# Row-wise maximum of absolute values over 8192 x 8192: groups of 48 and 16 rows per partition instead of 46 and 18, and the second group's results in one store

## The chip, the cores and the metric

The kernel runs on one core of a Trainium2 chip. The metric is the device time of one execution in microseconds (us), of which the median of several executions is taken. A profiled execution has a time of its own, and inside it a span from the first to the last instruction.

## The reference

```
x = randn(8192, 8192), float32
out = np.linalg.norm(x, ord=np.inf, axis=1)      # 8192 float32
```

For two-dimensional input with an axis given this is, for each row, the largest absolute value in the row: `out[i] = max over j of |x[i, j]|`. The input has 268.44 MB, the output 32 KiB. There is one comparison per element read, so the input passes through the core once and nothing is used twice.

## The kernel before

**Layout.** The 8192 rows are spread over 128 partitions, 64 rows to a partition. They are not spread in one piece: `GROUPS = [46, 18]` (L18) makes two groups. The first 46 x 128 rows of x belong to group one, where partition p holds the 46 neighbouring rows 46p to 46p+45; the last 18 x 128 rows belong to group two, with 18 neighbouring rows to a partition. The views are made at L47 to L50: `x_of` is a [128, k x 8192] view of x and `out_of` a [128, k] view of the output. A row has 8192 x 4 bytes = 32 KiB, so from one partition to the next a load moves on in memory by 46 x 32 KiB = 1472 KiB in group one and by 18 x 32 KiB = 576 KiB in group two. This distance is called the pitch below.

**Loads.** The 64 rows of a partition are taken in order, in the pieces that WHOLE (L21) and LAST (L24) list: two loads of one row (8192 elements for each partition), 29 of two rows (16384 elements, 64 KiB for each partition, 8 MiB in all), one of two rows and one of one row whose work is shared among engines, and then the last row in six pieces from 3920 down to 352 elements. All 39 loads are issued by SP at L108, in this order, into a ring of three 64 KiB places (RING, L27), the last piece into a tile of its own (`last`). A load waits until VectorE has finished with the place of the ring that it overwrites.

**Work.** VectorE (DVE) reduces each buffer with one `tensor_reduce` with absolute value and maximum (L68), which writes one or two columns of `res`, a [128, 64] tile with one column for each row of a partition. Towards the end (L133 to L136 and L146 to L150) a part of each buffer goes another way: ScalarE (ACT) replaces it by its absolute value in place (L90), and GpSimd (POOL) takes its maximum as integers (L75). The partial results are then joined, on POOL for rows 61 and 62 (L136), and on DVE for the last row (L153), which reads the last 352 elements and the nine partial results together.

**Stores.** After the last reduce three stores are issued. SP stores the last column alone, 4 bytes for each partition (L154, `final`). ACT stores columns 0 to 45 (184 bytes for each partition) and columns 46 to 62 (68 bytes for each partition) at L159; these two stand behind ACT's own absolute values in its queue. The dependency at L160 orders only the schedule, so that the early stores take the later semaphores; it adds no wait.

**Order.** `keep` holds each engine's instructions in program order. SP's queue has only the loads and then the final store.

Of the kernel before, what the change touches and what calls it, by code (L numbers as in the profile page):

```python
# [1 line left out]

# [4 lines left out]

P = 128
FP32 = mybir.dt.float32
INT32 = mybir.dt.int32  # L10
MAX = mybir.AluOpType.max
X = mybir.AxisListType.X
ABS = mybir.ActivationFunctionType.Abs

GROUPS = [46, 18]  # L18


WHOLE = (  # L21
    [(8192, ())] * 2 + [(16384, ())] * 29 + [(16384, (3712, 3680)), (8192, (2016, 1984))]
)
LAST = [  # L24
    (3920, (1680,)), (1984, (848,)), (1040, (432,)), (576, (240,)), (320, ()), (352, ())
]
RING = 3 * 16384  # L27


@with_exitstack  # L30
def kernel(
    ctx: ExitStack,
    tc: tile.TileContext,
    x: bass.AP,
    out: bass.AP,
):
    nc = tc.nc
    n_rows, n_cols = x.shape
    R = n_rows // P
    assert R == sum(GROUPS) and n_cols == 8192  # L40
    keep = tc.keep_in_program_order


    first = []
    x_of, out_of = {}, {}
    for k in GROUPS:
        f = len(first)  # L47
        x_of[f] = x[f * P : (f + k) * P].rearrange("(p r) m -> p (r m)", r=k)
        out_of[f] = out[f * P : (f + k) * P].rearrange("(p r) -> p r", r=k)
        first += [f] * k  # L50

    single = ctx.enter_context(tc.tile_pool(name="single", bufs=1))

    ring = single.tile([P, RING], FP32)
    res = single.tile([P, R], FP32)

    n_parts = sum(1 + len(g) for w, g in LAST[:-1])
    last = single.tile([P, LAST[-1][0] + n_parts], FP32)

    def not_before(inst, other, why):  # L60
        tc.add_manual_dep(
            inst.ins, other.ins.name,
            mybir.DependencyInfo(mybir.DependencyClass.Sync, mybir.DependencyReason.DATA),
            reason=why,
        )

    def absmax(dst, src):
        return keep(nc.vector.tensor_reduce(  # L68
            out=dst, in_=src, axis=X, op=MAX, apply_absolute_value=True,
        ))  # L70

    def max_pool(dst, src):

        pool = nc.gpsimd
        keep(pool.add_instruction(  # L75
            mybir.InstTensorReduce(
                name=nc.get_next_instruction_name(),
                ins=[pool.lower_ap(src.bitcast(INT32))],
                outs=[pool.lower_ap(dst.bitcast(INT32))],
                op=MAX,  # L80
                axis=X,
            )
        ))

    def shared(part, buf, g):

        a = buf.shape[1] - sum(g)
        red = absmax(part[:, :1], buf[:, :a])
        for i, c in enumerate(g):
            keep(nc.scalar.activation(buf[:, a : a + c], buf[:, a : a + c], ABS))  # L90
            max_pool(part[:, 1 + i : 2 + i], buf[:, a : a + c])
            a += c
        return red

    loads = []

    def load(pos, w):

        row = pos // n_cols
        a = pos - first[row] * n_cols  # L100
        if pos + w == R * n_cols:
            buf = last[:, :w]
        else:
            at = loads[-1][0] + loads[-1][1] if loads else 0
            if at + w > RING:
                at = 0
            buf = ring[:, at : at + w]
        inst = nc.sync.dma_start(out=buf, in_=x_of[first[row]][:, a : a + w]).ins  # L108
        if pos + w < R * n_cols:
            if (len(loads) + 4) % 10 < 5:  # L110


                for b, v, earlier in loads:
                    if b < at + w and at < b + v:
                        tc.declare_no_dep(
                            inst, earlier, reason="ordered by the reduces in between",
                        )
            loads.append((at, w, inst))
        return buf


    pos = 0
    for u, (w, g) in enumerate(WHOLE):
        buf = load(pos, w)
        row, k = pos // n_cols, w // n_cols
        pos += w
        whole = k - 1 if g else k
        if whole:
            red = absmax(
                res[:, row : row + whole],  # L130
                buf[:, : whole * n_cols].rearrange("p (c m) -> p c m", m=n_cols),
            )
        if g:  # L133
            part = single.tile([P, 1 + len(g)], FP32, name=f"part{u}")
            shared(part, buf[:, whole * n_cols :], g)
            max_pool(res[:, row + whole : row + k], part)  # L136
        if u == 1:

            not_before(
                keep(nc.scalar.activation(res[:, :1], res[:, :1], ABS)),  # L140
                red, "not before the second row is in",
            )


    n = LAST[-1][0]
    for h, (w, g) in enumerate(LAST[:-1]):  # L146
        buf = load(pos, w)
        pos += w
        shared(last[:, n : n + 1 + len(g)], buf, g)
        n += 1 + len(g)  # L150

    load(pos, LAST[-1][0])
    absmax(res[:, R - 1 :], last)  # L153
    final = nc.sync.dma_start(out=out_of[first[-1]][:, GROUPS[-1] - 1 :], in_=res[:, R - 1 :])  # L154


    for f, o in out_of.items():
        k = min(o.shape[1], R - 1 - f)
        early = keep(nc.scalar.dma_start(out=o[:, :k], in_=res[:, f : f + k]))  # L159
        tc.add_manual_dep(  # L160
            early.ins, final.ins.name,
            mybir.DependencyInfo(
                mybir.DependencyClass.NoSync, mybir.DependencyReason.SCHED_ONLY
            ),
            reason="takes the later semaphore",
        )


# [1 line left out]
_INS = ['x']  # L170
_OUTS = [((8192,), 'float32')]


# [23 lines left out]
```

## Time and profile before

| | us |
|---|---|
| median of 4 runs (627.40 to 627.47) | 627.42 |
| the profiled execution, its own time | 627.38 |
| its span, first to last instruction | 625.6 |
| outside its span | 1.78 |
| DVE busy | 536.7 |
| ACT busy | 15.1 |
| POOL busy | 14.1 |

The page gives each engine's busy time and its share of the span, the DMA queues with the bytes that they moved, a chain of waits followed back from the last instruction, groups of instructions with the mean time of one and the idle time before them, and for DMA issues the time from issue to landing. Queue q1 is SP's, q10 is ACT's. The landing time of a load holds the time that it stood behind earlier loads. A table by stretches of time gives busy time, DMA share and GB/s for each stretch; a DMA share of 1.00 says that all 16 DMA engines were busy throughout.

### The profile page before, as it was taken

Reading aid. Unit: us, or ns where it says so; the run is one execution under the profiler, and the core shown is the slowest. Engines: PE = TensorE matmul, PEld = TensorE weight load, DVE = VectorE, ACT = ScalarE, POOL = GpSimd, SP = SyncE. Lnnn points to the kernel's source line nnn. Section 1 sums busy time; section 2 is a strip of 40 time slices with the busy share of each in tenths; the row PEclk is TensorE's granted clock in tenths of the full one; section 3 lists DMA queues with packets and bytes.
Section 4 is the critical chain, followed back from the end, with each engine's and each line's share of the span. In section 5 each row is a group of like instructions: output and inputs, shape, how many; then the busy total and the mean of one; then the engine's idle time right before and its main releaser. Section 6 shows DMA issues by size and latency. Waiting matters only on the chain.

```text
span 625.6 us, 175 instructions
## 1 busy us (share of the span) xinstructions
DVE 536.7 (86%) x40; ACT 15.1 (2%) x10; POOL 14.1 (2%) x14
## 2 busy tenths in 40 slices
DVE  1938988889888899888898888988889888899888
ACT  0000000000000000000000000000000000000044
POOL 0000000000000000000000000000000000000026
DMA  8999999999999999999999999999999999999997
GB/s 369 436 469 402 469 402 469 402 469 402 469 402 448 423 406 465 402 469 402 469 402 469 402 469 402 469 402 440 432 402 469 402 469 402 469 402 469 402 436 304
DMA packets 6048, 268.47 MB, mean 429 GB/s; under 512 B 1056, under 2 KB 1312, under 8 KB 1696
## 3 DMA queue, kind: packets, MB, share of 16 engines
q1 hardware_dynamic: 5760, 268.44, 99.3%
q10 hardware_dynamic: 288, 0.03, 0.0%
HBM read 268.44 MB, written 0.03 MB: 429 GB/s over the span
## 4 chain that ended last, share of the span: by engine, by line
DMA 71%; DVE 28%; SPq 0%; issue 0%; DVEq 0%
DMA ring<-in_x_dram 71%; DVE res L68 28%; DVE last L68 1%; SPq L108 0%; DVEq L68 0%
## 5 line engine op out<-in xcount | busy, mean ns | idle before, releaser
L68 DVE TENSOR_REDUCE res<-ring 128x2 f32<-128x16384 f32 (+1 forms) x32 | 525.4, 16420 | 86.3 <-DMA ring<-in_x_dram 86.3
L90 ACT ACTIVATE ring<-ring 128x3712 f32<-128x3712 f32 (+7 forms) x8 | 13.6, 1719 | 577.2 <-DMA ring<-in_x_dram 573.9
L75 POOL TENSOR_REDUCE part<-ring 128x1 int32<-128x3712 int32 (+3 forms) x4 | 10.1, 2561 | 607.6 <-ACT ring L90 607.6
L68 DVE TENSOR_REDUCE part<-ring 128x1 f32<-128x800 f32 (+1 forms) x2 | 5.5, 2748 | 0.1
L68 DVE TENSOR_REDUCE last<-ring 128x1 f32<-128x2240 f32 (+4 forms) x5 | 5.3, 1115 | 0.1
L75 POOL TENSOR_REDUCE last<-ring 128x1 int32<-128x1680 int32 (+3 forms) x4 | 3.4, 854 | 0.6 <-ACT ring L90 0.4
L140 ACT ACT_TABLE_LOAD x1 | 1.3, 1283 | 0.7 <-PEq L181 0.7
L140 ACT ACTIVATE res<-res 128x1 f32<-128x1 f32 x1 | 0.2, 203 | 29.2 <-DVE res L68 29.2
L68 DVE TENSOR_REDUCE res<-last 128x1 f32<-128x361 f32 x1 | 0.5, 529 | 0.1
L75 POOL TENSOR_REDUCE res<-part 128x1 int32<-128x3 int32 x2 | 0.4, 197 | 0.1
L181 POOL MEMSET const-float32-0.0<- 128x1 f32 x1 | 0.1, 98 | 0.2 <-issue 0.2
L181 POOL MEMSET const-bfloat16-1.0<- 128x1 bf16 x1 | 0.1, 101 | 0.0
L181 POOL MEMSET const-uint8-127<- 128x1 uint8 x1 | 0.1, 101 | 0.0
L181 POOL MEMSET const-float32-1.0<- 128x1 f32 x1 | 0.1, 98 | 0.0
## 6 DMA issues: line engine op xcount, KB each, us to landing
ring<-in_x_dram SPq DMA_DIRECT2D x3, 4096.0 KB, 21.3
ring<-in_x_dram SPq DMA_DIRECT2D x1, 1960.0 KB, 35.4
ring<-in_x_dram SPq DMA_DIRECT2D x1, 992.0 KB, 37.4
ring<-in_x_dram SPq DMA_DIRECT2D x1, 520.0 KB, 38.2
ring<-in_x_dram SPq DMA_DIRECT2D x30, 40.8
ring<-in_x_dram SPq DMA_DIRECT2D x1, 288.0 KB, 38.4
last<-in_x_dram SPq DMA_DIRECT2D x1, 176.0 KB, 38.3
ring<-in_x_dram SPq DMA_DIRECT2D x1, 160.0 KB, 38.3
```

The source lines that it names most:

```text
L68: return keep(nc.vector.tensor_reduce(out=dst, in_=src, axis=X, op=MAX, apply_absolute_value=True,))
L75: keep(pool.add_instruction(mybir.InstTensorReduce(name=nc.get_next_instruction_name(), ins=[pool.lower_ap(src.bitcast(INT32))], outs=[poo ...
L90: keep(nc.scalar.activation(buf[:, a : a + c], buf[:, a : a + c], ABS))
L140: keep(nc.scalar.activation(res[:, :1], res[:, :1], ABS)),
L181: nc = _bacc.Bacc("TRN2", target_bir_lowering=False, num_devices=1)
```

## The change

The groups become 48 and 16 rows for each partition. The pitch of a load becomes 48 x 32 KiB = 1536 KiB in group one and 16 x 32 KiB = 512 KiB in group two. The list of loads, the ring and all reduces keep their sizes; only which rows of x a partition holds, and so the addresses in memory, are others. The border between the groups lies behind row 47 of a partition instead of behind row 45.

The three stores become two. SP stores all 16 columns of the second group after the last reduce, 64 bytes for each partition, which lie one after another in the output without a gap (8 KiB). ACT stores the 48 columns of the first group, 192 bytes for each partition. The store of columns 46 to 62 is gone.

```diff
-GROUPS = [46, 18]
+GROUPS = [48, 16]
...
     load(pos, LAST[-1][0])
     absmax(res[:, R - 1 :], last)
-    final = nc.sync.dma_start(out=out_of[first[-1]][:, GROUPS[-1] - 1 :], in_=res[:, R - 1 :])
 
 
-    for f, o in out_of.items():
-        k = min(o.shape[1], R - 1 - f)
-        early = keep(nc.scalar.dma_start(out=o[:, :k], in_=res[:, f : f + k]))
-        tc.add_manual_dep(
-            early.ins, final.ins.name,
-            mybir.DependencyInfo(
-                mybir.DependencyClass.NoSync, mybir.DependencyReason.SCHED_ONLY
-            ),
-            reason="takes the later semaphore",
-        )
+
+    f, g = first[0], first[-1]
+    final = nc.sync.dma_start(out=out_of[g], in_=res[:, g:])
+    early = keep(nc.scalar.dma_start(out=out_of[f], in_=res[:, f:g]))
+    tc.add_manual_dep(
+        early.ins, final.ins.name,
+        mybir.DependencyInfo(mybir.DependencyClass.NoSync, mybir.DependencyReason.SCHED_ONLY),
+        reason="takes the later semaphore",
+    )
```

## The prediction

> **What bounds the kernel now.** I read the page from the top first: busy times, the DMA queues, the chain of waits.
>
> ```profile
> span 625.6 us, 175 instructions
> DVE 536.7 (86%) x40; ACT 15.1 (2%) x10; POOL 14.1 (2%) x14
> ...
> q1 hardware_dynamic: 5760, 268.44, 99.3%
> q10 hardware_dynamic: 288, 0.03, 0.0%
> ...
> DMA ring<-in_x_dram 71%; DVE res L68 28%; DVE last L68 1%; SPq L108 0%; DVEq L68 0%
> ```
>
> VectorE is busy for 86% of the span, but the packets of SP's queue fill 99.3% of the time of 16 DMA engines. The chain changes between a load and a reduce because a load needs a free place in the ring; which of the two is the bound is seen in the groups of instructions, kept apart by shape:
>
> ```profile
> L68 DVE TENSOR_REDUCE res<-ring 128x2 f32<-128x16384 f32 x29 | 499.4, 17220 | 70.3 <-DMA ring<-in_x_dram 70.3
> ```
>
> A two-row reduce takes 17.22 us, and each waits some 2.1 us for its load. Reduces follow one another every 19.35 us, at the loads' pace. The table by stretches, three reduces to a stretch, gives that pace in three stretches of group one (46 rows) and then in the stretch that holds the first loads of group two (18 rows):
>
> ```profile
> 117.17:175.22 58.05, 51.66 (x3) 0.00 (x0) 0.00 (x0) 1.00 1.00 434
> 175.22:233.27 58.05, 51.66 (x3) 0.00 (x0) 0.00 (x0) 1.00 1.00 434
> 233.27:291.32 58.05, 51.66 (x3) 0.00 (x0) 0.00 (x0) 1.00 1.00 434
> ...
> 466.10:524.15 58.05, 51.66 (x3) 0.00 (x0) 0.00 (x0) 1.00 1.00 434
> ```
>
> Three loads are 3 x 8.389 MB = 25.17 MB in 58.05 us, 433.5 GB/s, with a DMA share of 1.00. The two-row reduces start at 41.87 us with row 2 and go on by 19.35 us a pair, so that rows 46 and 47, group two's first, are reduced from 41.87 + 22 x 19.35 = 467.6 us. The rate is the same on both sides. So the kernel is a stream at one rate from start to end, and then a tail, which the timeline shows:
>
> ```profile
> 621.11 1.10 ACT L90 ACTIVATE ring<-ring 128x432 f32<-128x432 f32 x2 [0.37 <-DMA ring<-in_x_dram]
> 621.81 0.86 ACTq L159 DMA_DIRECT2D out_dram<-res  x2
> 622.80 0.53 DVE L68 TENSOR_REDUCE res<-last 128x1 f32<-128x361 f32 x1
> 623.35 0.35 SPq L154 DMA_DIRECT2D out_dram<-res  x1
> ```
>
> The last reduce ends at 623.33, SP issues the last store at 623.35, and the span ends at 625.6. The list of DMA issues gives the three stores' times to landing:
>
> ```profile
> out_dram<-res ACTq DMA_DIRECT2D x1, 23.0 KB, 1.6
> out_dram<-res ACTq DMA_DIRECT2D x1, 8.5 KB, 1.6
> out_dram<-res SPq DMA_DIRECT2D x1, 0.5 KB, 1.4
> ```
>
> The last one lands at 623.35 + 1.4 = 624.75; the remaining 0.85 us is the program's closing.
>
> **What the Trainium skill says.** Four places bear on this, all in "DMA: Bandwidth & Descriptors".
> - "Where 436 GB/s comes from" puts the ceiling of the 16 ports at 435.2 GB/s. The trace agrees: 433.5, and a DMA share of 1.00.
> - "Latency and other measured facts" has a row on the row pitch at large powers of two. Copies from memory to memory of [128 x 16 KiB] tiles ran at 214 GB/s in each direction when the pitch was padded by 4 KiB, at 207 with a pitch of 512 KiB, at 164 with 2 MiB and 103 with 4 MiB. It calls the cause (streams in lock step meeting in the same channels) an inference. The trace of before can neither confirm nor deny it: its pitches are 1472 KiB = 23 x 64 KiB and 576 KiB = 9 x 64 KiB, neither a large power of two, and both run at 434.
> - "The descriptor swizzle" gives each engine blocks of four neighbouring partitions, so that neighbouring engines read four pitches apart. No view here shows it.
> - "Specifications" has transfers below 512 B done by reading and rewriting. All stores here, before and after, are below that (4, 68 and 184 bytes; then 64 and 192), so the page offers no gain to the 64 bytes.
>
> **The change, part by part.**
>
> *Loads with another pitch.* The 39 loads, their bytes, their order and SP's waits stay as they are; no instruction is added or moved here. What may change is the rate. The pitch becomes 1536 KiB = 3 x 512 KiB for 48 of the 64 rows and 512 KiB for 16, so all the traffic now has 512 KiB as the power of two in its pitch, where before it had 64 KiB. Nothing covers a loss: DVE already waits 2.1 us for each load, so a load that takes longer lengthens the run by the whole difference. The stream is 268.44 MB / 433.5 GB/s = 619.2 us, so one per cent of rate is 6.2 us. The upper end comes from the skill's row: 214/207 = 1.034, that is 0.034 x 619.2 = +20.9 us. The lower end: the rate may rise at most from 433.5 to the stated 435.2, 0.4%, -2.4 us. I take 0. The reason is that the row's loss is for copies, in which the same engines read and write memory at the same pitch; at 2 MiB they still moved 164 + 164 = 328 GB/s in both directions together and at 512 KiB 414, with both sides aliased. A load has only its reading side in memory, half as many streams, and at 512 KiB the row's loss has almost faded. Against this: 414 is less than the 434 that the load needs, so the row doesn't exclude a loss, and I give that nearly the same chance.
>
> *The border behind row 47.* One load of rows 46 and 47 comes from group one instead of two. No load crosses a border. 0.
>
> *Reduces.* Same shapes, same number, other rows: 0. DVE's 17.22 us against 19.35 us covers 2.13 us anyway.
>
> *ACT's stores, two to one.* The two issues take 0.86 us of ACT's queue from 621.81; one remains, so ACT is done some 0.43 us earlier (622.24). Nothing stands behind it. The stores landed by 622.24 + 1.6 = 623.8 at the latest, before SP's at 624.75. Off the path: 0. One store fewer must be waited for at the close; the closing semaphore steps on SP take 17 to 28 ns each, so at most -0.03 us.
>
> *SP's store, 4 to 64 bytes for each partition.* It waits for the same last reduce; it now waits also for POOL's results for rows 61 and 62, the later of which is in at 618.47 + 0.20 = 618.67, 4.7 us before. Nothing stands behind it on SP. As before it has 128 pieces, so the issue of 0.35 us stays. Its time to landing is bounded by the rows that surround it: 1.4 us at 4 bytes and 1.6 at 68 and 184, so 0 to +0.2. A gain below zero would need 64 bytes to land sooner than 4; as the landing 1.4 is mostly fixed, I let it go to -0.1. I take +0.1.
>
> *Sum.* On the profiled execution's own time: 627.38 (span 625.6 and 1.78 outside) + 0 + 0.1 = 627.48, rounded to 627.5. The profiled execution lies 0.04 below the median of 627.42, which is less than the rounding.
>
> **Rivals.**
>
> *Part of the pitch's loss shows (slower).* Place: every load. If a copy's 3.4% is the sum of what its two aliased sides lose, a load loses 1.7%: 0.017 x 619.2 = 10.5 us, 637.9 us. For it: the DMA engines have no slack (share 1.00), and all 39 loads have the pitch. Against: the two directions of a copy may disturb one another, which a load doesn't know. It decides as soon as memory gives the 16 engines less than 433.5 GB/s together; above that it is worth nothing.
>
> *The whole of it or more (slower).* If memory gives only what the copies had in both directions together at 512 KiB, 414 GB/s or a little more, the loss is 3.4 to 4.7%. With the row's ratio: 627.4 + 20.9 = 648.3 us. For it: 64 KiB are read in one piece from each partition, so streams remain in step for long. Against: as above.
>
> *Faster stream.* The new addresses let the rate reach 435.2: 627.4 - 2.4 = 625.0 us. Against: nothing in the trace shows a rate that depends on the pitch, and 0.4% is all there is.
>
> *The tail turns out otherwise.* The 64-byte store could land 0.2 later or 0.1 sooner: 627.3 to 627.6. This stays within the forecast.
>
> **How the numbers follow.** A difference of 0.2% (1.25 us) is about what a measurement of this kernel can tell from no change. Only the tail moves: 0.48, 627.5 us. Part of the loss: 0.26, around 637.9, from 629 to 643. The whole or more: 0.23, around 648.3 and beyond. Faster stream: 0.03. So faster 0.03, same 0.48, slower 0.26 + 0.23 = 0.49. The likeliest case has the range 626.9 to 628.4 of its own: from -0.1 in the landing and a rate better by 0.07%, to +0.2 and a rate worse by 0.1%. The range for 8 in 10 begins at 626.9, which leaves out the faster stream, and must reach into the third case: up to 648.3 it leaves out half of that, 0.115, so 0.145 in all. The slower cases together hold as much as the likeliest; they are spread over 20 us, which it is not.
>
> **What would show it.** The stretches of three reduces: 58.05 us and 434 GB/s if the pitch costs nothing; 59.0 and 426 in the second case; 60.0 and 419 in the third. DVE's wait before a two-row reduce: 2.13 us, against 2.46 and 2.79. If the two pitches differ, the stretch length jumps at row 48, 41.87 + 23 x 19.35 = 486.9 us. In the tail, the distance from the end of the last reduce to the end of the span: 2.27 us now, 2.2 to 2.5 expected; SP's store 1.4 to 1.6 to landing, and one ACT store. The prediction is wrong if the stretches are longer than 58.2 us with a DMA share of 1.00, or if a wait of SP on something other than the reduces appears between loads.

## The result and the profile after

The changed kernel takes 628.15 us (median of 34 runs, 627.93 to 628.49) against 627.44 us for the kernel before (52 runs, 627.34 to 627.73). The ratio is 1.0011, with a 95% interval of 1.0006 to 1.0016: slower by 0.7 us. This is clear of the noise, though it is less than the 0.2% that the prediction took for about the least that can be told from no change. The profiled execution took 628.23 us with a span of 626.5 us; before it was 627.38 and 625.6. So there are 0.9 us of span to be found.

The page after, its head and the queues:

```profile
span 626.5 us, 174 instructions
DVE 536.7 (86%) x40; ACT 15.0 (2%) x10; POOL 14.1 (2%) x14
...
q1 hardware_dynamic: 5760, 268.45, 99.3%
q10 hardware_dynamic: 144, 0.02, 0.0%
```

The work is the same; q10, ACT's queue, has half the packets because one of its two stores is gone. The first place to look is the rate. These are the same stretches of time as in the prediction (length, then busy time and count of DVE, ACT and POOL, clock, DMA share, GB/s):

```profile
117.17:175.22 58.05, 51.66 (x4) 0.00 (x0) 0.00 (x0) 1.00 1.00 434
175.22:233.27 58.05, 51.66 (x4) 0.00 (x0) 0.00 (x0) 1.00 1.00 434
233.27:291.32 58.05, 51.65 (x4) 0.00 (x0) 0.00 (x0) 1.00 1.00 434
466.10:524.15 58.05, 51.66 (x4) 0.00 (x0) 0.00 (x0) 1.00 1.00 434
```

434 GB/s in both groups, as before. (A count of x4 only says that a stretch cuts reduces at both ends.) The end of the run is as long as before: from the end of the last reduce, 624.18, to the end of the span there are 2.3 us, before 2.27.

```profile
623.65 0.53 DVE L68 TENSOR_REDUCE res<-last 128x1 f32<-128x361 f32 x1
624.20 0.35 SPq L158 DMA_DIRECT2D out_dram<-res  x1
```

The list of DMA issues shows the two stores, KB and us to landing:

```profile
out_dram<-res ACTq DMA_DIRECT2D x1, 24.0 KB, 1.5
out_dram<-res SPq DMA_DIRECT2D x1, 8.0 KB, 1.4
```

Sixteen times as many bytes land in the same 1.4 us. What is left is the start. The timeline of VectorE, before (start, duration, instruction, idle time ahead of it and what ended it):

```profile
12.83 8.69 DVE L68 TENSOR_REDUCE res<-ring 128x1 f32<-128x8192 f32 x1 [12.83 <-DMA ring<-in_x_dram]
22.51 8.69 DVE L68 TENSOR_REDUCE res<-ring 128x1 f32<-128x8192 f32 x1 [1.00 <-DMA ring<-in_x_dram]
41.87 17.22 DVE L68 TENSOR_REDUCE res<-ring 128x2 f32<-128x16384 f32 x1 [10.67 <-DMA ring<-in_x_dram]
```

and after:

```profile
13.58 8.69 DVE L68 TENSOR_REDUCE res<-ring 128x1 f32<-128x8192 f32 x1 [13.58 <-DMA ring<-in_x_dram]
23.26 8.69 DVE L68 TENSOR_REDUCE res<-ring 128x1 f32<-128x8192 f32 x1 [1.00 <-DMA ring<-in_x_dram]
42.62 17.22 DVE L68 TENSOR_REDUCE res<-ring 128x2 f32<-128x16384 f32 x1 [10.68 <-DMA ring<-in_x_dram]
62.09 17.22 DVE L68 TENSOR_REDUCE res<-ring 128x2 f32<-128x16384 f32 x1 [2.25 <-DMA ring<-in_x_dram]
```

The first load lands 13.58 - 12.83 = 0.75 us later, and the second and third are late by the same 0.75. The fourth adds 2.25 - 2.13 = 0.12. The last reduce starts at 623.65 instead of 622.80, 0.85 later: nothing further is lost in 560 us. The whole difference is made by the first four loads, nearly all of it by the very first, and it is never won back, because the stream behind it has no slack.

The packet records of the two traces, which hold start, duration and size of each piece that a DMA engine moved, narrow this down. A packet of the first load carries the 32 KiB of one partition, and the first sixteen packets all begin before any of them has ended. The last of these sixteen ends at 3.97 us before and at 4.73 after. That is 0.76 us later, so the whole delay of the first load is already there at the end of its first packets.

**Theory:** the new pitch costs a fixed amount while the stream starts and nothing once it runs. A possible reason is that the 16 DMA engines begin in step, meet in memory at such a pitch, and drift apart. **Rivals:** the stores cost it; or the pitch costs whenever the engines come to it; or it costs a little all the time.

### The profile page after: what moved, and what is told of

Its sections match the earlier page's. It is cut to its first block, busy times and chain, and to the rows that moved or that the text cites. A ratio compares the mean times of both kernels' runs of the same rounds, so it can differ in the third digit from the quotient of the medians.

```text
span 626.5 us, 174 instructions
## 1 busy us (share of the span) xinstructions
DVE 536.7 (86%) x40; ACT 15.0 (2%) x10; POOL 14.1 (2%) x14
## 4 chain that ended last, share of the span: by engine, by line
DMA 71%; DVE 28%; SPq 0%; issue 0%; DVEq 0%
DMA ring<-in_x_dram 71%; DVE res L68 28%; DVE last L68 1%; SPq L108 0%; DVEq L68 0%
## 5 line engine op out<-in xcount | busy, mean ns | idle before, releaser
L90 ACT ACTIVATE ring<-ring 128x3712 f32<-128x3712 f32 (+7 forms) x8 | 13.6, 1719 | 577.3 <-DMA ring<-in_x_dram 574.0
```

## The experiments

Each cut shows what a kernel has in place of the changed kernel's lines, except in the second experiment, which starts from the kernel before. In kernels with other groups SP stores the last group at the end and ACT each other group with a store of its own; the lines for this are left out of the cuts.

**The stores alone.** The groups stay 46 and 18; the stores are those of the change.

```diff
-GROUPS = [48, 16]
+GROUPS = [46, 18]
```

> Groups of 46 and 18 as before, stores as after (one store of the second group at the end, 72 bytes per partition here). Theory: the 0.7 us are lost in the first loads, through the pitch; so this is as before, 627.4 (within 0.1), and the third load's reduce starts at 41.9. Rival: the later or bigger last store costs it; then 628.1.

627.46 us against 627.40 for before on the same chip, ratio 1.0001 (0.9993 to 1.0009). The first reduce starts as early as in the kernel before, and the last store lands in 1.4 us:

```profile
12.73 8.69 DVE L68 TENSOR_REDUCE res<-ring 128x1 f32<-128x8192 f32 x1 [12.73 <-DMA ring<-in_x_dram]
```

```profile
out_dram<-res SPq DMA_DIRECT2D x1, 9.0 KB, 1.4
```

The stores are not the cause.

**The groups alone.** Before's three stores, with the new groups.

```diff
-GROUPS = [46, 18]
+GROUPS = [48, 16]
```

> Groups of 48 and 16, three stores as before (last column alone). Theory (pitch, in the first loads): as after, 628.1, the third load's reduce starts at 42.5 or later, stretches of three reduces stay 58.05. Rival (stores): 627.4.

628.08 us, ratio 1.0011 (1.0004 to 1.0017): all of the change's cost. The first reduce is late by 0.57, the fifth waits 2.31 instead of 2.13:

```profile
13.40 8.69 DVE L68 TENSOR_REDUCE res<-ring 128x1 f32<-128x8192 f32 x1 [13.40 <-DMA ring<-in_x_dram]
...
81.33 17.22 DVE L68 TENSOR_REDUCE res<-ring 128x2 f32<-128x16384 f32 x1 [2.31 <-DMA ring<-in_x_dram]
```

The third load's reduce starts at 42.45, a little before the 42.5 that was expected.

**512 KiB in the first 16 rows alone.**

```diff
-GROUPS = [48, 16]
+GROUPS = [16, 30, 18]
```

> Groups of 16, 30 and 18 rows: pitch 512 KiB for the first 16 rows alone, then 960 KiB = 15 x 64 KiB and 576 KiB; 18 columns stored at the end. Theory (cold start: only the first loads pay): the first load's reduce starts 0.5 to 0.8 us later than before's 12.83, nothing more is lost later, 628.0 to 628.2. Rival (1536 KiB with its own pattern costs, 512 KiB does not): 627.4.

628.14 us, ratio 1.0011 (1.0005 to 1.0018). The first reduce starts at 13.42, the third load's at 42.47, and every later two-row reduce waits 2.12 to 2.14 us.

```profile
13.42 8.69 DVE L68 TENSOR_REDUCE res<-ring 128x1 f32<-128x8192 f32 x1 [13.42 <-DMA ring<-in_x_dram]
```

So 512 KiB and 3 x 512 KiB cost about the same at the start (0.59 us here, 0.57 and 0.75 above), and a quarter of the rows at that pitch costs as much as all of them.

**1536 KiB from row 14 on.**

```diff
-GROUPS = [48, 16]
+GROUPS = [14, 48, 2]
```

> Groups of 14, 48 and 2 rows: pitch 448 KiB = 7 x 64 KiB for the first 14 rows, 1536 KiB from row 14 on; the last group's two columns are stored at the end. Theory (cold start: the pitch costs only while all engines begin in step): 627.4, third load's reduce at 41.9. Rival (the engines pay once whenever they come to a pitch of a large power of two): the start is as before, some 0.8 us are lost between rows 14 and 20 (120 to 200 us), 628.1. Second rival (steady small loss): stretches over 58.1 from row 14 on, more than 628.1.

628.83 us, ratio 1.0023 (1.0015 to 1.0031), 1.4 more than the theory expected. But the stream did what the theory said. The timeline, first reduce, the first two of rows 14 to 17 and the last one:

```profile
12.81 8.69 DVE L68 TENSOR_REDUCE res<-ring 128x1 f32<-128x8192 f32 x1 [12.81 <-DMA ring<-in_x_dram]
...
157.95 17.22 DVE L68 TENSOR_REDUCE res<-ring 128x2 f32<-128x16384 f32 x1 [2.13 <-DMA ring<-in_x_dram]
177.30 17.22 DVE L68 TENSOR_REDUCE res<-ring 128x2 f32<-128x16384 f32 x1 [2.13 <-DMA ring<-in_x_dram]
...
622.81 0.53 DVE L68 TENSOR_REDUCE res<-last 128x1 f32<-128x361 f32 x1
```

The last reduce starts at 622.81, before's at 622.80. 48 rows at 1536 KiB cost nothing once the stream runs; both rivals on the loads fall. The loss of this kernel is behind the last reduce, in the list of DMA issues:

```profile
out_dram<-res SPq DMA_DIRECT2D x1, 1.0 KB, 2.7
```

A store of 8 bytes for each partition, which lie in the output without gaps, took 2.7 us to landing, where 4 bytes 72 bytes apart had taken 1.4. That was a side effect of the third group, and it needed runs of its own.

**The 8-byte store behind other loads.**

```diff
-GROUPS = [48, 16]
+GROUPS = [46, 16, 2]
```

> Groups of 46, 16 and 2 rows, the last group's two columns stored at the end, 8 bytes per partition without gaps. Theory for the end of the run with groups of 14, 48 and 2 (the store of short neighbouring pieces takes 2.7 us to landing where 4 bytes 72 bytes apart and 64 or 72 bytes without gaps take 1.4): the same 2.7 here, 627.4 + 1.3 = 628.7. Rival (its long landing came from the loads' pitch before it): 1.4 and 627.4. The 512 KiB of rows 46 to 61 cost nothing in either.

628.82 us, ratio 1.0022 (1.0014 to 1.0031), with 2.9 us to landing, so the 1536 KiB ahead of the store was not the cause. In both kernels the last two rows have the pitch 64 KiB, which this pair can't part from the store; a run below does so for 4 bytes.

**32 bytes instead of 8.**

```diff
-GROUPS = [48, 16]
+GROUPS = [46, 10, 8]
```

> Groups of 46, 10 and 8 rows; the last group's eight columns are stored at the end, 32 bytes per partition without gaps. Theory (stores without gaps cost the more, the more partitions fall into one short stretch of memory: 4 bytes 7.5 us, 8 bytes 2.8, 64 bytes 1.4): 1.4 to 2.0 us to landing, 627.4 to 628.0. Rival (anything below 64 bytes without gaps costs over a us): 2.5 us or more, over 628.5.

627.42 us, ratio 1.0000 (0.9991 to 1.0008), 1.4 us to landing. Pieces of 32 bytes side by side are as good as 64 or 72.

**4 bytes side by side, at the end and early.** One group of one row in front.

```diff
-GROUPS = [48, 16]
+GROUPS = [1, 45, 18]
```

> Groups of 1, 45 and 18 rows: the first load has the pitch 32 KiB, without a gap between partitions; then 1440 KiB = 45 x 32 KiB. 18 columns stored at the end. Theory (the cold start is a question of the first load's addresses): if a pitch with a smaller power of two starts better, the first reduce begins before 12.7 and the time is 627.0 to 627.3; if before's start has no loss from the pitch, as before, 627.4. Rival (neighbouring pieces collide more): over 627.6.

633.63 us, ratio 1.0099 (1.0085 to 1.0113): far over the rival's 627.6, and for the most part not in the loads. The start is worse than before's by 0.3 (first reduce at 13.13), and some 6 us are lost in the stores:

```profile
out_dram<-res ACTq DMA_DIRECT2D x1, 22.5 KB, 8.2
out_dram<-res ACTq DMA_DIRECT2D x1, 0.5 KB, 7.6
out_dram<-res SPq DMA_DIRECT2D x1, 9.0 KB, 7.5
```

All three are slow, so the list alone doesn't say which one holds up the others. Moving the 4-byte store ahead does (the cut is against the kernel just shown):

```diff
+            f0 = GROUPS[0]
+            keep(nc.scalar.dma_start(out=out_of[0], in_=res[:, :f0]))
...
-        if f == g:
+        if f in (0, g):
             continue
```

> Groups of 1, 45 and 18 rows again, but the first column's store, 4 bytes per partition without gaps, is issued at some 31 us under the loads and not at the end. Theory (that store's 4-byte neighbours took the 7.5 us at the end of the run, and held up the other two stores): the end is short again, last store 1.4 us to landing, 627.5 to 627.9 (the first reduce at 13.1). Rival (the other stores, 180 and 72 bytes, or the odd pitch are the cause): 7 us or more to landing again, 633.6.

629.66 us, ratio 1.0035 (1.0022 to 1.0048). At the end, the stores land in 1.5 and 1.4 us again, so the 4-byte store was the cause. The expected 627.5 to 627.9 was missed all the same, because under the loads the store is not free. The third and fourth loads' reduces:

```profile
42.91 17.22 DVE L68 TENSOR_REDUCE res<-ring 128x2 f32<-128x16384 f32 x1 [11.35 <-DMA ring<-in_x_dram]
63.87 17.22 DVE L68 TENSOR_REDUCE res<-ring 128x2 f32<-128x16384 f32 x1 [3.73 <-DMA ring<-in_x_dram]
```

They wait 11.35 and 3.73 us, where the kernel with the store at the end had 10.67 and 2.12: 2.3 us of load time lost to a store of 512 bytes. (The profiled execution, 630.05 us, is the slowest of the five.)

**Two rows at 64 KiB in front of 1536 KiB.** The same early store, here with 8 bytes for each partition.

```diff
-GROUPS = [48, 16]
+GROUPS = [2, 48, 14]
```

> Groups of 2, 48 and 14 rows: the first two loads have the pitch 64 KiB, and 1536 KiB begins with the third load. The first group's two columns are stored by ACT at some 31 us, under the loads; 14 columns at the end. Theory (only the first load of all pays for a large power of two): the first reduce starts at 12.7 to 13.2 and nothing is lost at the third load, 627.3 to 627.8. Rival (the engines pay at the first loads of the large pitch, when they still run in step from the start): the third load's reduce starts 0.5 to 0.8 later than the first load's start alone explains, 628.0 to 628.6.

629.13 us, ratio 1.0029 (1.0017 to 1.0040), outside what either theory said. The first reduce starts well, at 12.77; the third load's is late:

```profile
42.96 17.22 DVE L68 TENSOR_REDUCE res<-ring 128x2 f32<-128x16384 f32 x1 [11.79 <-DMA ring<-in_x_dram]
```

It waits 1.12 us longer than before's (10.67). The 8-byte store is issued in the same stretch, at 31.4, and the 4-byte one was just seen to delay the same load. So this run doesn't tell whether the pitch costs something at the third load; it is inconclusive by its own design.

**A larger power of two.** 1024 KiB, then 2048 KiB throughout.

```diff
-GROUPS = [48, 16]
+GROUPS = [32, 32]
```

> Groups of 32 and 32 rows: pitch 1024 KiB throughout, stores as after. Theory: the loss at the start grows with the power of two in the pitch, 1 to 3 us, 628.4 to 630.5, and stretches stay at 58.05 to 58.2. Rival (memory can no longer feed the stream at this pitch): stretches of 59 us and more, 635 to 660.

639.80 us (four runs, 637.98 to 640.38), ratio 1.0192 (1.0178 to 1.0206). This lies in the rival's range, not in the theory's. The stretches are slow first and right at last:

```profile
0.00:46.77 46.77, 17.37 (x2) 1.49 (x2) 0.20 (x4) 1.00 0.99 381
46.77:227.51 180.74, 154.98 (x10) 0.00 (x0) 0.00 (x0) 1.00 1.00 421
227.51:401.66 174.15, 154.97 (x9) 0.00 (x0) 0.00 (x0) 1.00 1.00 432
401.66:575.81 174.15, 154.98 (x9) 0.00 (x0) 0.00 (x0) 1.00 1.00 434
```

The second stretch, 421 GB/s, has a DMA share of 1.00 too: the share says that the engines had packets, not that these moved at full rate. This stretch holds nine reduces, 60.2 us for three, so the rival was right about it. By the last stretch the pitch of 1024 KiB runs at 434, so memory can deliver at it; that the loss fades after the start is nearer to the theory.

```diff
-GROUPS = [48, 16]
+GROUPS = [64]
```

> One group of 64 rows, pitch 2048 KiB throughout; one store of 256 bytes per partition at the end. Theory (the loss grows with the power of two in the pitch: 0.7 us at 512 KiB, 12.4 at 1024): 30 to 150 us over before, 657 to 780, with a loss in every stretch and no longer only at the start. Rival (a load, which has memory on one side only, drifts apart as at 1024 KiB): 640 to 655, the loss in the first third.

639.83 us (four runs, 637.45 to 641.41), ratio 1.0193 (1.0174 to 1.0213). The theory's dose, 657 to 780, is wrong: 2048 KiB costs the same as 1024, at the lower end of the rival's range. But the loss lies elsewhere than in the rival's first third. In the profiled execution, the slowest of the four, the third load's reduce starts 4.7 us later than before's, the last two-row reduce 8.5 later (592.20 against 583.68) and the last reduce of all 13.95 later (636.75 against 622.80). Four stretches up to 569 us have 385, 428, 430 and 431 GB/s, and then the pieces of the last row come late:

```profile
626.52 2.49 DVE L68 TENSOR_REDUCE last<-ring 128x1 f32<-128x2240 f32 x1 [0.53 <-DMA ring<-in_x_dram]
631.12 1.33 DVE L68 TENSOR_REDUCE last<-ring 128x1 f32<-128x1136 f32 x1 [2.11 <-DMA ring<-in_x_dram]
633.58 1.59 DVE L68 TENSOR_REDUCE last<-ring 128x1 f32<-128x608 f32 x3 [1.12 <-DMA ring<-in_x_dram]
636.75 0.53 DVE L68 TENSOR_REDUCE res<-last 128x1 f32<-128x361 f32 x1 [1.58 <-DMA last<-in_x_dram]
```

Before, these reduces followed one another without a wait. The packet records show that the packets themselves are slow here: the 128 packets of the last load, 1408 bytes each, take 0.22 us on average and up to 1.07, against 0.06 in the kernel before and at 1024 KiB. These packets also end far apart, within 7.2 us here against 0.7 before and 1.4 after the change. That alone is not the reason, since at 1024 KiB they end within 7.3 us and the last reduces have no such waits.

**An uneven start at 1024 KiB.** ACT issues small loads that nothing uses, to 8, 4, 2 and 1 partitions, at the start.

```diff
+    for i, n in enumerate((8, 4, 2, 1)):
+        keep(nc.scalar.dma_start(
+            out=ring[:n, 32768 + i * 4096 : 36864 + i * 4096], in_=x[:n, :4096],
+        ))
```

> Groups of 32 and 32 (1024 KiB), but ACT first issues four small loads of 16 KiB for each of 8, 4, 2 and 1 partitions that nothing uses, so that some DMA engines begin the real loads up to some 2.4 us behind the others. Theory (the loss comes from engines that run in step, and fades as they drift apart): less is lost than with even engines, 630 to 637 instead of 639.8, though the extra loads cost 0.6 to 2.4 by themselves. Rival (the pitch itself limits what memory gives, in step or not): 640 to 642.

638.36 us (five runs, 635.42 to 639.93), ratio 1.0169 (1.0149 to 1.0189), between what the theory and the rival said. The timeline, first and last reduce:

```profile
18.59 8.69 DVE L68 TENSOR_REDUCE res<-ring 128x1 f32<-128x8192 f32 x1 [18.59 <-DMA ring<-in_x_dram]
...
633.57 0.53 DVE L68 TENSOR_REDUCE res<-last 128x1 f32<-128x361 f32 x1
```

The extra loads delay the first reduce far more than was reckoned, from 14.04 to 18.59 us. From the first to the last reduce it is 614.98 us here, 621.57 (14.04 to 635.61) with even engines, and 609.97 (12.83 to 622.80) in the kernel before. So 5.0 us are lost there instead of 11.6. This does not decide. The runs of the two kernels overlap (635.42 to 639.93 against 637.98 to 640.38), and what the even kernel loses later may here have moved under the first load. The edit also didn't do quite what it was meant to: both queues begin to issue at 0.74 us, so the small loads run beside the first real load and not ahead of it. Nor does the rate rise as with even engines: in the three later stretches of the table above this kernel has 430, 431 and 431 GB/s, where even engines had 421, 432 and 434.

## Why the prediction was right, point by point

The forecast was 627.5 us, no change within 0.2%; it is 628.15. The sum was 0.7 us short, and the term that was mis-sized is **the loads with another pitch**, "I take 0".

- *What bounds the kernel*: right, and it is why 0.75 us at the start arrive whole at the end. "Nothing covers a loss" was the sentence that counted.
- *The loads*: the price was set as a share of the rate over all 619 us, from 0 to 3.4%. The rate did not move: 58.05 us and 434 GB/s in all four stretches. In place of a rate there was a fixed cost at the first load, 0.75 us in the profile and 0.57 with the groups alone. Both kernels with the new groups have it (628.08 and 628.15), both with the old ones don't (627.46 and 627.44). The 0.12 at the fourth load can't be put down to the pitch: the kernel with groups of 46, 16 and 2, in its profiled execution, lost 0.19 and 0.26 us at two loads of the pitch 1472 KiB. The reason given for 0, that a load has memory on one side only, fits the steady rate, though no run tests it against another; it said nothing about a start. The first load's own row, 12.1 us to landing where the steady stream would need 4.19 MB / 433.5 GB/s = 9.7, was in the trace and would have shown that the start has a price of its own.
- *The range*: that 628.15 lies within the likeliest case's 626.9 to 628.4 is in part luck. That margin was made of a rate worse by 0.1% and a landing later by 0.2 us, and neither came. The forecast was also a near thing: 0.48 for no change, 0.49 for slower.
- *The skill's row on the pitch*: for copies, "DMA: Bandwidth & Descriptors", section "Latency and other measured facts", has 164 GB/s at 2 MiB against 214 padded, a quarter less. Loads at 2048 KiB here lost 1.9% of the whole run. The measurement decides: the row's figures don't carry over to loads like these. That 1024 and 2048 KiB cost time at all agrees with it.
- *The two slower rivals*: neither came. Their prices, 10.5 and 20.9 us, belonged to a rate that would have stayed low; not even 2048 KiB reached 627.4 + 20.9.
- *The faster stream*: no sign of it.
- *ACT's stores*: right. The early store lands in 1.5 us, ahead of SP's; ACT's saving is not on the path.
- *SP's store*: +0.1 was taken, within -0.1 to +0.2. The landing stayed at 1.4, and the stores alone, with 72 bytes in place of 64, measured 1.0001 (0.9993 to 1.0009), which can't be told from 0.
- *The distance to the end*: 2.2 to 2.5 were expected, 2.3 were found.

Shown: the cost comes with the groups and not with the stores; it lies in the start of the stream; 1536 KiB later in the run costs nothing. The packet records put it in the first packets: the last of the first sixteen ends at 4.57 to 4.73 us in the three kernels that begin with 512 or 1536 KiB, and at 3.90 to 4.01 in the six that begin with 64, 448 or 1472. The two that begin with 32 KiB have 4.30 and 4.35. The first reduce is late by the same amounts, within 0.05 us.

Argued, and not shown: that the engines collide while they run in step. Open: why the first packets are late, and whether a pitch of 1536 KiB costs anything at the third load, since the run meant for it was spoilt by its own store. The first load doesn't rank by the power of two in its pitch alone either: first reduces at 12.7 to 12.9 us with 64, 448 and 1472 KiB, 13.1 to 13.2 with 32 KiB, 13.4 to 13.6 with 512 and 1536, 14.0 with 1024 and 14.9 with 2048.

## What to carry to other kernels

Before pricing a new memory layout as a rate, ask whether it acts on the running stream or on its start: a stream without slack carries a late first load to the end, whole and once. Look at the first load's landing apart from the steady interval, and when a DMA share is 1.00, read the GB/s beside it. Put results that are only a few bytes for each partition where their neighbours don't lie side by side in memory, or store more columns at once; 32 bytes for each partition were enough here.

## What the runs showed of the hardware that was not expected

- Stores of very short pieces that lie side by side: 4 bytes for each of 128 partitions took 7.6 us to landing, and two other stores issued beside it took 7.5 and 8.2; 8 bytes took 2.7 and 2.9; 32, 64 and 72 bytes took 1.4. 4 bytes at a distance of 72 or 64 took 1.4 as well, so it is not the size of the piece alone.
- The 4-byte store under running loads cost these 2.3 us.
- At a pitch of 1024 KiB most of the loss falls in the first 230 us, and the stream then reaches 432 and 434 GB/s. At 2048 KiB stretches of 174 us stay at 428 to 431, and the 1408-byte packets of the last load take 0.22 us instead of 0.06.
- A pitch of 512 or 1536 KiB costs 0.6 to 0.8 us in the first sixteen packets of the run. 1536 KiB costs nothing in the loads from row 14 on.
